# Counting VectorE's semaphore steps over a whole lap, and waiting for loads by a register, in a streaming mean-subtraction kernel

## The chip, the cores and the metric

One core of a Trainium2 chip. The metric is the device time of one execution in microseconds (us), of the slowest core; here there is one core. Three chips were used; the kernel before took 1285.1 to 1285.3 us (medians) on each.

## The reference

```python
B, S, D = 8, 4096, 2112          # x: float32, 276.8 MB
x_r = x.reshape(B, S // 4, 4, D)
pooled = x_r.mean(axis=2)
return (x - np.repeat(pooled, 4, axis=1)).astype(np.float32)
```

From every group of four rows its mean row is subtracted. All of x is read once and as many bytes are written.

## The kernel before

A tile is 128 groups, one per partition, 4 x 2112 = 8448 fp32 columns, 4.325 MB. There are 64 tiles and six SBUF slots. SyncE issues the loads; VectorE adds the four rows in three steps into a sum tile (in SBUF and PSUM by turns), then one wide instruction computes rows - sum/4 in place; ScalarE issues the stores. A load for a slot waits for the slot's store of the lap before.

```python
def reduce_tile(b, parity):
    rows = slots[b].rearrange("p (f d) -> p f d", f=STRIDE)
    s = s_ps if parity else s_sb
    add = nc.vector.tensor_add(out=s[:], in0=rows[:, 0, :], in1=rows[:, 1, :])   # L60
    add._wait_ge(load_sems[b], 16)
    add.then_inc(load_sems[b], -16)          # taken back
    add = nc.vector.tensor_add(out=s[:], in0=s[:], in1=rows[:, 2, :])            # L63
    add.wait_op(load_sems[b], 0, "sem-eq")
    add.then_inc(step_sem)
    add = nc.vector.tensor_add(out=s[:], in0=s[:], in1=rows[:, 3, :])            # L66
    add._wait_ge(step_sem, 1)
    add.then_inc(step_sem, -1)               # taken back
    sub = nc.vector.scalar_tensor_tensor(out=rows, ...)                          # L69
    sub.wait_op(step_sem, 0, "sem-eq")
    sub.then_inc(done_sem)
# ... cut: loads as k = 0..63 on SyncE ...
with nc.vector.Fori(0, laps):                # 10 laps of 6 tiles, then 4 tiles
    for b in range(SLOTS):
        reduce_tile(b, b % 2)
# ... cut: stores on ScalarE, store k waits for done_sem >= k + 1 ...
```

## Time and profile before

| | before |
|---|---|
| time, median of the first 3 runs | 1285.18 us (1285.16 to 1285.22) |
| span of the profiled run | 1283.3 us |
| VectorE busy | 1026.5 us, 80% |
| loads and stores, time of their packets as a share of 16 DMA engines | 50.1% + 50.0% |
| period of a tile in the steady state | 19.97 us |
| VectorE's chain for one tile, from landing to the end of the wide instruction | 16.3 us |

### The profile page before, as it was taken

The numbers are of one execution on the slowest core, as the hardware profiler recorded it, in microseconds if no ns is written. First come the engines' busy times: TensorE is split into PE (matmuls) and PEld (weight loads), VectorE is DVE, ScalarE is ACT, GpSimd is POOL, SyncE is SP. The second block draws the span as 40 slices with busy tenths as digits, with TensorE's granted clock in tenths as the row PEclk, the third lists the DMA queues.
The fourth block names the chain that finished last, engine by engine and source line by source line (L and its number), as shares of the span: only waits on it lengthen the run. The fifth ranks groups of instructions, "written<-read, shape, count | busy, mean of one in ns | idle before, by whom it ended". The sixth has DMA issues, their size and how long they took to land.

```text
span 1283.3 us, 591 instructions
## 1 busy us (share of the span) xinstructions
DVE 1026.5 (80%) x256; POOL 0.2 (0%) x4
## 2 busy tenths in 40 slices
DVE  5998788787787877878778787787887878878775
POOL 0000000000000000000000000000000000000000
DMA  9999999999999999999999999999999999999999
GB/s 404 421 437 433 428 438 432 428 438 437 431 430 438 432 428 438 437 429 432 438 432 428 438 436 429 433 438 432 428 438 435 429 434 438 432 428 438 434 427 404
DMA packets 18433, 553.66 MB, mean 431 GB/s; under 512 B 2048, under 2 KB 2048, under 8 KB 2048
## 3 DMA queue, kind: packets, MB, share of 16 engines
q1 hardware_dynamic: 9216, 276.83, 50.1%
q10 hardware_dynamic: 9216, 276.83, 50.0%
q14 instruction: 1, 0.01, 0.0%
HBM read 276.82 MB, written 276.82 MB: 431 GB/s over the span
## 4 chain that ended last, share of the span: by engine, by line
DVE 71%; another core or an unknown queue 23%; issue 3%; DMA 1%; DVEq 0%; SPq 0%
DVE slot L69 36%; DVE s_ps L66 6%; DVE s_ps L60 6%; DVE s_ps L63 6%; DVE s_sb L66 6%; DVE s_sb L63 6%; DVE s_sb L60 6%; DMA slot<-in_x_dram 1%; DVEq L66 0%; DVEq L60 0%; DVEq L90 0%; SPq L131 0%; SPq L82 0%
## 5 line engine op out<-in xcount | busy, mean ns | idle before, releaser
L69 DVE SCALAR_TENSOR_TENSOR slot<-s_sb,slot 128x8448 f32<-128x8448 f32 x32 | 286.6, 8957 | 1.1
L69 DVE SCALAR_TENSOR_TENSOR slot<-s_ps,slot 128x8448 f32<-128x8448 f32 x32 | 286.6, 8957 | 1.1
L60 DVE TENSOR_TENSOR s_sb<-slot 128x2112 f32<-128x2112 f32 x32 | 75.4, 2357 | 121.7 <-DMA slot<-in_x_dram 121.7
L60 DVE TENSOR_TENSOR s_ps<-slot 128x2112 f32<-128x2112 f32 x32 | 75.7, 2366 | 109.2 <-DMA slot<-in_x_dram 109.2
L66 DVE TENSOR_TENSOR s_ps<-s_ps,slot 128x2112 f32<-128x2112 f32 x32 | 75.7, 2367 | 3.3
L66 DVE TENSOR_TENSOR s_sb<-s_sb,slot 128x2112 f32<-128x2112 f32 x32 | 75.5, 2358 | 3.3
L63 DVE TENSOR_TENSOR s_ps<-s_ps,slot 128x2112 f32<-128x2112 f32 x32 | 75.7, 2366 | 1.1
L63 DVE TENSOR_TENSOR s_sb<-s_sb,slot 128x2112 f32<-128x2112 f32 x32 | 75.4, 2358 | 1.1
L120 POOL MEMSET const-bfloat16-1.0<- 128x1 bf16 x1 | 0.1, 102 | 0.0
L120 POOL MEMSET const-uint8-127<- 128x1 uint8 x1 | 0.1, 101 | 0.0
L120 POOL MEMSET const-float32-0.0<- 128x1 f32 x1 | 0.1, 99 | 0.2 <-issue 0.2
L120 POOL MEMSET const-float32-1.0<- 128x1 f32 x1 | 0.1, 98 | 0.0
## 6 DMA issues: line engine op xcount, KB each, us to landing
slot<-in_x_dram SPq DMA_DIRECT2D x64, 4224.0 KB, 59.7
out_dram<-slot ACTq DMA_DIRECT2D x64, 4224.0 KB, 43.7
```

The lines of the kernel that those rows point to most:

```text
L60: add = nc.vector.tensor_add(out=s[:], in0=rows[:, 0, :], in1=rows[:, 1, :])
L63: add = nc.vector.tensor_add(out=s[:], in0=s[:], in1=rows[:, 2, :])
L66: add = nc.vector.tensor_add(out=s[:], in0=s[:], in1=rows[:, 3, :])
L69: sub = nc.vector.scalar_tensor_tensor(out=rows, in0=s[:, None, :].to_broadcast([P, STRIDE, D]), scalar=-1.0 / STRIDE, in1=rows, op0=mybir ...
L120: nc = _bacc.Bacc("TRN2", target_bir_lowering=False, num_devices=1)
```

## The change

The intent is to have nothing to take back in a tile. The step counter only rises during a lap (18 adds) and is reduced once at its end; the load semaphores only rise, and the first add waits for a value that a register holds for the lap. The core of the diff:

```diff
-    def reduce_tile(b, parity):
+    def reduce_tile(b, landed):
...
-        add._wait_ge(load_sems[b], 16)
-        add.then_inc(load_sems[b], -16)
-        ... three adds written out, the third with then_inc(step_sem, -1)
+        done = b * adds                      # adds = 3
+        for f in range(1, STRIDE):
+            first = rows[:, 0, :] if f == 1 else s[:]
+            add = nc.vector.tensor_add(out=s[:], in0=first, in1=rows[:, f, :])
+            if f == 1:
+                add._wait_ge(load_sems[b], landed)
+            else:
+                add._wait_ge(step_sem, done + f - 1)
+            add.then_inc(step_sem)
-        sub.wait_op(step_sem, 0, "sem-eq")
+        sub._wait_ge(step_sem, done + adds)
...
-        with nc.vector.Fori(0, laps):
+        with nc.vector.Fori(0, laps) as lap:
+            landed = nc.vector.to_reg(16 * lap + 16)
             for b in range(SLOTS):
-                reduce_tile(b, b % 2)
+                reduce_tile(b, landed)
+            nc.vector.wait_ge(step_sem, SLOTS * adds).then_inc(step_sem, -SLOTS * adds)
```

More of the change, by code (lines that the diff above doesn't have):

```diff
@@ L31 @@
     G = (B * S) // STRIDE
-    assert STRIDE == 4 and S % STRIDE == 0 and G % P == 0
+    assert S % STRIDE == 0 and G % P == 0
     n = G // P
@@ L53 @@
     done_sem = tc.alloc_semaphore("done")
-    def reduce_tile(b, parity):
+    adds = STRIDE - 1
+    def reduce_tile(b, landed):
         rows = slots[b].rearrange("p (f d) -> p f d", f=STRIDE)
-        s = s_ps if parity else s_sb
-        add = nc.vector.tensor_add(out=s[:], in0=rows[:, 0, :], in1=rows[:, 1, :])
-        add._wait_ge(load_sems[b], 16)
-        add.then_inc(load_sems[b], -16)
-        add = nc.vector.tensor_add(out=s[:], in0=s[:], in1=rows[:, 2, :])
-        add.wait_op(load_sems[b], 0, "sem-eq")
-        add.then_inc(step_sem)
-        add = nc.vector.tensor_add(out=s[:], in0=s[:], in1=rows[:, 3, :])
-        add._wait_ge(step_sem, 1)
-        add.then_inc(step_sem, -1)
+        s = s_ps if b % 2 else s_sb
+        done = b * adds
[7 more added lines that the diff above has]
+            add.then_inc(step_sem)
         sub = nc.vector.scalar_tensor_tensor(
@@ L88 @@
             load.then_inc(load_sems[b], 16)
-        with nc.vector.Fori(0, laps):
+        with nc.vector.Fori(0, laps) as lap:
+            landed = nc.vector.to_reg(16 * lap + 16)
             for b in range(SLOTS):
-                reduce_tile(b, b % 2)
+                reduce_tile(b, landed)
+            nc.vector.wait_ge(step_sem, SLOTS * adds).then_inc(step_sem, -SLOTS * adds)
         for b in range(rest):
-            reduce_tile(b, b % 2)
+            reduce_tile(b, 16 * (laps + 1))
         for k in range(n):
```

## The prediction

> **What bounds the kernel now.** I read the page from the top: busy shares, slices, DMA queues. 64 tiles of 128 x 8448 fp32 pass through six slots; SyncE issues loads, VectorE (DVE) does three adds and one wide multiply-add, ScalarE issues stores.
>
> ```profile
> span 1283.3 us, 591 instructions
> ## 1 busy us (share of the span) xinstructions
> DVE 1026.5 (80%) x256; POOL 0.2 (0%) x4
> ...
> DMA  9999999999999999999999999999999999999999
> ...
> q1 hardware_dynamic: 9216, 276.83, 50.1%
> q10 hardware_dynamic: 9216, 276.83, 50.0%
> ```
>
> VectorE is busy 80% of the span. The DMA row is 9 in all 40 slices, and the two rings (q1 loads, q10 stores) together take 100.1% of the time of 16 DMA engines. That is the first sign that transfers are the bound. Occupancy of 16 engines can mislead, so I check the rate. The starts of the first add in two steady tiles 32 apart (613.31 and 1252.19 us on the timeline) give a period of 638.88 / 32 = 19.965 us. In it one tile of 4.325 MB is loaded and one is stored: 8.651 MB / 19.965 us = 433 GB/s.
>
> Next, the groups of instructions: what VectorE waits for.
>
> ```profile
> L60 DVE TENSOR_TENSOR s_sb<-slot 128x2112 f32<-128x2112 f32 x32 | 75.4, 2357 | 121.7 <-DMA slot<-in_x_dram 121.7
> L60 DVE TENSOR_TENSOR s_ps<-slot 128x2112 f32<-128x2112 f32 x32 | 75.7, 2366 | 109.2 <-DMA slot<-in_x_dram 109.2
> L66 DVE TENSOR_TENSOR s_ps<-s_ps,slot 128x2112 f32<-128x2112 f32 x32 | 75.7, 2367 | 3.3
> ```
>
> Ahead of each tile's first add (L60) VectorE stands idle for the load, 121.7 + 109.2 = 230.9 us in all; the other three instructions of a tile wait for next to nothing. One steady tile in the chain of waits:
>
> ```profile
> 609.53 3.68 another core or an unknown queue
> 613.21 0.03 issue
> 613.24 0.02 DVEq L60
> 613.26 0.04 issue
> 613.31 2.38 DVE s_ps L60
> 615.68 0.02 issue
> 615.71 2.38 DVE s_ps L63
> 618.08 0.03 issue
> 618.11 0.02 DVEq L66
> 618.13 0.04 issue
> 618.18 2.38 DVE s_ps L66
> 620.55 0.02 issue
> 620.58 8.96 DVE slot L69
> ```
>
> The page's chain puts 71% on VectorE, which invites the wrong conclusion. The chain alternates: 16.3 us of VectorE, then 3.68 us with no name. The group lines name it: the load. So VectorE has about 3.7 us of slack in every 19.97 us. Its work sits in the chain because a tile does pass through it, but the pace is set by the transfers. A closed loop of six slots could also be limited by latency, not by rate: with nothing queued a tile would need about 12.4 us of load (the fastest landing), 16.3 us of VectorE and 13.9 us of store (the fastest landing), 42.6 us in all, or 7.1 us per tile over six slots. The period is 19.97 us, so the slots are not short; the medians of 59.7 us (load) and 43.7 us (store) from issue to landing are mostly queueing. Both rings always hold work.
>
> **The two ends** must be looked at apart, for there a later VectorE could show. At the head six loads are queued at once, about 60 us of transfer, and the first store is issued at 29.7 us: the engines never run dry. At the tail the windows of 2 us show:
>
> ```profile
> 1266.00:1268.00 2.00, 2.00 (x1) 0.00 (x0) 1.00 1.21 524
> 1268.00:1270.00 2.00, 0.42 (x1) 0.00 (x0) 1.00 0.86 372
> 1270.00:1272.00 2.00, 0.00 (x0) 0.00 (x0) 1.00 1.06 456
> ```
>
> The last two columns are the DMA share and GB/s. The last store is issued at 1268.4 us, when VectorE ends, and lands 13.9 us later. Alone at 433 GB/s it would need 4.325 MB / 433 = 10.0 us, so about 3.9 us of other stores (and completion) still stand ahead of it. The rate does not dip before it joins. A last store issued a little earlier only queues.
>
> [...]
>
> **The change part by part.** *Removed*: two take-backs per tile (load semaphore by 16, step semaphore by 1) and the equality waits for them. The trace has a separate 21 ns semaphore instruction ahead of L60 and of L66, x64 each. The gap before L66 is 0.03 + 0.02 + 0.04, about 0.10 us by start times (618.18 - 618.08); that before L63 or L69, without one, is 0.02 to 0.03. One is worth about 0.07 us, two 0.15 us a tile, 64 tiles 9.6 us of VectorE time. *Added*: in each of ten laps a register value, a wait for 18 adds and a subtraction of 18. The instruction order shows one more instruction at the lap's start and a wait merged into the loop's register step. Register steps of the loop take 40 ns and its branch 56 ns now; three or four such are some 0.2 us a lap, 2 us in all. They can run beside the lap's last wide instruction (8.96 us), because the last add is done before that starts. Each first add now compares against a register[...]. *Unchanged*: the four VectorE instructions, all 128 DMAs, slots, store waits, 553.66 MB.
>
> VectorE's sum: -9.6 + (0 to 2)[...] = -9.6 to -1.2 us of time not counted as busy. The tile goes from 16.28 to about 16.15 us. All of this is inside 3.7 us of slack, so the wait for the load grows by as much: 230.9 us becomes 232 to 241 us. On the path that sets the end: 0. At the head stores are issued 0.1 to 0.7 us earlier and meet a busy queue: 0.
>
> **The rivals.** (1) *VectorE's time is on the path*, as the 71% suggests: then 9.6 us come off, 1275.6 us, 0.7% and still within 2%. Against it: idle for the load ahead of 59 of 64 first adds, full DMA in all slices. (2) *The new wait replaces the old ones and costs more*: a register wait, or a lap's end that drains VectorE. It would have to exceed 3.7 us per tile, or build up beyond the slack and the queue, to show; even 1 us fully exposed in each of ten laps makes 1295 us, under 1%. Nothing in the trace takes that long on the sequencer: 21 to 56 ns apiece. (3) *Shifted stores change how loads and stores mix*, hence the DMA rate. The slices scatter between 428 and 438 GB/s by turns, averaging 433; an overall shift of 0.1% (1.3 us) is thinkable either way, with nothing in favour of a direction.
>
> **Range and chances.** The transfers set the time, so I take 1285.1 us. Three runs lie within 0.06 us, so the range comes from rival 3 and a small share of rival 1: 1284.2 to 1286.0 us. For 2% the time must move 25.7 us, over twice what the whole saving could give and far more than the lap's work could cost. Chances: faster 0.005, within 2% 0.985, slower 0.01.
>
> **What would show it.** Right: DMA share still 9 everywhere, 433 GB/s steady, period 19.97 us; no semaphore instruction ahead of the first and third add; the gap before the third add down from 0.10 to about 0.03 us; VectorE still 1026.5 us busy; its load waits up by 1 to 10 us; span 1283 us. Wrong: a period that moves with VectorE's chain (rival 1), a sequencer gap of microseconds at each lap's first add (rival 2), or the same bytes at another rate (rival 3).

Cut from the prediction is what no trace or run showed: the term for a first add that compares against a register. VectorE's sum came to -9.6 to -1.2 us with that term; the terms left, -9.6 and 0 to 2, come to -9.6 to -7.6 us. The lower ends of "232 to 241 us" and "up by 1 to 10 us" hold the cut term too: without it the wait for loads would become 238.5 to 240.5 us, 7.6 to 9.6 us more. The 1285.1 us does not rest on it, for the prediction counts all of VectorE's time as slack. That the adds keep their length is shown by the pages: the groups' means are 2357 to 2367 ns before and 2358 to 2367 ns after.

## The result, and the profile after

The changed kernel took 1284.87 us (median of 6 runs, 1284.78 to 1285.14), the kernel before 1285.20 us in 6 runs. The ratio is 0.9998, 95% interval 0.9985 to 1.0011: the same. (Ratios here are the mean time of one kernel's fast runs over that of the other's fast runs of the same rounds, so not quite the ratio of the medians quoted.)

The page of the changed kernel:

```profile
span 1283.3 us, 483 instructions
## 1 busy us (share of the span) xinstructions
DVE 1026.5 (80%) x256; POOL 0.2 (0%) x4
...
DMA  9999999999999999999999999999999999999999
...
q1 hardware_dynamic: 9216, 276.83, 50.1%
q10 hardware_dynamic: 9216, 276.83, 50.0%
```

108 instructions fewer than before (591), the same busy time, the same span, the same two DMA queues (called rings below: q1 carries the loads, q10 the stores) at 100% of the engines.

The groups, with the last two fields being busy us with mean ns, and idle us ahead with what ended it:

```profile
L63 DVE TENSOR_TENSOR s_sb<-slot 128x2112 f32<-128x2112 f32 x32 | 75.5, 2358 | 123.7 <-DMA slot<-in_x_dram 123.7
L63 DVE TENSOR_TENSOR s_ps<-slot 128x2112 f32<-128x2112 f32 x32 | 75.7, 2367 | 112.1 <-DMA slot<-in_x_dram 112.1
L63 DVE TENSOR_TENSOR s_ps<-s_ps,slot 128x2112 f32<-128x2112 f32 x64 | 151.4, 2366 | 2.2
```

The wait for the load is 123.7 + 112.1 = 235.8 us, 4.9 us more than before.

One steady tile of the changed kernel in the chain of waits (start, us, what), the same tile as the prediction shows of before:

```profile
609.98 3.81 another core or an unknown queue
613.79 0.02 issue
613.81 2.38 DVE s_ps L63
616.19 0.02 issue
616.21 2.38 DVE s_ps L63
618.59 0.02 issue
618.61 2.38 DVE s_ps L63
620.99 0.02 issue
621.01 8.96 DVE slot L69
```

The two DVEq pieces of 0.02 us, the separate semaphore instructions, are gone. From the end of the wait to the end of the wide instruction the tile takes 629.97 - 613.79 = 16.18 us, against 629.54 - 613.21 = 16.33 us: 0.15 us saved. The wait in front of it grew from 3.68 to 3.81 us. The saving is real and the load takes it back in the same tile.

The absolute times hold something more. This first add starts at 613.81 us, *later* than 613.31 us before, although VectorE became faster. The start of the run shows where that sets in. Before:

```profile
29.60 2.36 DVE L60 TENSOR_TENSOR s_ps<-slot 128x2112 f32<-128x2112 f32 x1
...
85.23 8.96 DVE L69 SCALAR_TENSOR_TENSOR slot<-s_sb,slot 128x8448 f32<-128x8448 f32 x1
94.22 2.37 DVE L60 TENSOR_TENSOR s_ps<-slot 128x2112 f32<-128x2112 f32 x1
```

After:

```profile
29.38 2.36 DVE L63 TENSOR_TENSOR s_ps<-slot 128x2112 f32<-128x2112 f32 x1
...
84.73 8.96 DVE L69 SCALAR_TENSOR_TENSOR slot<-s_sb,slot 128x8448 f32<-128x8448 f32 x1
94.73 2.37 DVE L63 TENSOR_TENSOR s_ps<-slot 128x2112 f32<-128x2112 f32 x1 [1.04 <-DMA slot<-in_x_dram]
```

In the first five tiles VectorE does not wait for loads, and its gain adds up: the fifth wide instruction begins 0.50 us earlier (84.73 against 85.23), so stores start earlier. Yet the sixth tile's first add, which hardly waited before, now waits 1.04 us and begins 0.51 us later (94.73 against 94.22), and from there every load is complete 0.6 us later.

It is tempting to say that the earlier stores pushed the loads back, but the trace does not bear that out. Averaged over the time from 300 to 1200 us, the bytes moved so far are the same in both kernels: 168.26 MB of loads against 168.30 before, 155.05 MB of stores in each. The trace records 16 completions for every transfer (2048 for 128 transfers). Midway, the first of a load's 16 comes at 632.71 us against 632.68 before; the last comes 1.04 us after it instead of 0.49, with the other fifteen within 0.53. So one completion of the 16 comes half a microsecond behind the others (633.75 us, the one ahead of it 633.24), and VectorE waits for the last: its first add starts at 633.77 us. Whether the change causes this is not shown: there is one profile of each kernel, and two variants of the changed kernel in experiment 4 (1.8 us after the wide instruction, 0.5 us in the chain) have no such straggler.

The last store is issued at 1268.9 instead of 1268.4 us and lands 13.5 instead of 13.9 us later. The end stays.

### The profile page after: what moved, and what is told of

Read it like the earlier page. It is cut to its first block, busy times and chain, and to the rows that moved or that the text cites. A ratio compares the mean times of both kernels' runs of the same rounds, so it can differ in the third digit from the quotient of the medians.

```text
span 1283.3 us, 483 instructions
## 1 busy us (share of the span) xinstructions
DVE 1026.5 (80%) x256; POOL 0.2 (0%) x4
## 2 busy tenths in 40 slices
DMA packets 18432, 553.66 MB, mean 431 GB/s; under 512 B 2048, under 2 KB 2048, under 8 KB 2048
## 3 DMA queue, kind: packets, MB, share of 16 engines
q1 hardware_dynamic: 9216, 276.83, 50.1%
## 4 chain that ended last, share of the span: by engine, by line
DVE 73%; another core or an unknown queue 24%; DMA 1%; issue 1%; DVEq 0%; SPq 0%
DVE slot L69 38%; DVE s_ps L63 18%; DVE s_sb L63 18%; DMA slot<-in_x_dram 1%; DVEq L90 0%; SPq L133 0%; SPq L82 0%
## 5 line engine op out<-in xcount | busy, mean ns | idle before, releaser
L63 DVE TENSOR_TENSOR s_sb<-slot 128x2112 f32<-128x2112 f32 x32 | 75.5, 2358 | 123.7 <-DMA slot<-in_x_dram 123.7
L63 DVE TENSOR_TENSOR s_ps<-slot 128x2112 f32<-128x2112 f32 x32 | 75.7, 2367 | 112.1 <-DMA slot<-in_x_dram 112.1
L63 DVE TENSOR_TENSOR s_sb<-s_sb,slot 128x2112 f32<-128x2112 f32 x64 | 150.9, 2358 | 2.2
```

What stands on the lines that cost most here:

```text
L63: add = nc.vector.tensor_add(out=s[:], in0=first, in1=rows[:, f, :])
```

## The experiments

Twelve kernels were run. The theory: the transfers set the time, and VectorE's gain disappears in its wait for loads. Rival 1: VectorE's chain is on the path, as the chain view's 73% of the changed kernel suggests. (Rival 2 of the prediction, a costly register wait, is tested in experiment 3; rival 3, another DMA rate, comes up in experiment 4.) Diffs are shortened. "Wrong result" below means a kernel that was meant to compute something else.

### 1. VectorE's work taken away (wrong result)

```diff
-  tensor_add(out=s[:], in0=first, in1=rows[:, f, :])      # and the wide instruction over 8448 columns
+  tensor_add(out=s[:, :8], in0=..., in1=rows[:, f, :8])   # and the wide instruction over 4 x 8
```

> The changed kernel with all four VectorE instructions cut to 8 columns (wrong result on purpose): same loads, stores, waits and order, but VectorE's chain per tile falls from 16.2 us to about 1 us. Theory (the transfers set the time): the time stays at 1284 to 1286 us; the first store starts near 15 us instead of 29.5 us, the loads then share the engines from earlier on, so the last load lands 10 to 20 us later than 1252.6 us, and the end does not move. Rival 1 (VectorE's chain is on the path, as its 73% share of the chain suggests): about 15 us per tile come off, or at least 15 us at the two ends: 1270 us or far less.

Measured: 1285.49 us (median of 4, 1285.01 to 1285.92), ratio 1.0001. VectorE was busy 45.0 us instead of 1026.5 us, and the time did not move. The timeline of this kernel, first and last tile:

```profile
14.15 77.37 ACTq L100 DMA_DIRECT2D out_dram<-slot  x5
...
1269.40 0.18 DVE L63 TENSOR_TENSOR s_ps<-slot 128x8 f32<-128x8 f32 x1 [19.19 <-DMA slot<-in_x_dram]
```

The first store is issued at 14.15 us, 15.4 us earlier than in the changed kernel (29.50 us); the last first add begins at 1269.40 us, 16.7 us later than there (1252.69 us). What stores gain, loads lose: averaged from 300 to 1200 us, the stores have moved 3.50 MB more than in the changed kernel and the loads 3.55 MB less, and the end stays. Rival 1 falls.

### 2. Fewer bytes, the same VectorE work (wrong result)

```diff
-  store = nc.scalar.dma_start(out=og[k * P:(k + 1) * P], in_=slots[b][:])
+  store = nc.scalar.dma_start(out=og[k * P:(k + 1) * P, :3 * D], in_=slots[b][:, :3 * D])
```

> The changed kernel with each store cut to three of the four rows of a group (wrong result on purpose): VectorE does the same work, the bytes fall by one eighth, 69.2 MB. Theory: the time falls by 69.2 MB / 433 GB/s = 160 us, to about 1125 us (1115 to 1140), a period of 17.5 us, with VectorE's tile of 16.16 us still inside it. Rival 1: the time does not move by more than a few us.

Measured: 1128.18 us, ratio 0.878. An eighth of the bytes less, 12.2% of the time less. The stores' ring fell to 42.8% of 1126.3 us = 482 us of all engines, three quarters of the 642 us (50.0% of 1283.3) that it had. Time goes with bytes.

### 3. VectorE made the bound, and the two parts of the change one by one (wrong results)

In these four, loads after the first lap and all stores move two of the four rows, about 10 us per tile. The first is the kernel before, the second the changed kernel; the third and fourth carry one part of the change each:

```diff
# all four
-  load = nc.sync.dma_start(out=slots[b][:], in_=xg[k * P:(k + 1) * P])
+  wide = 2 * D if lap else W
+  load = nc.sync.dma_start(out=slots[b][:, :wide], in_=xg[k * P:(k + 1) * P, :wide])   # store: :2 * D
# third: steps counted over the lap (two per tile), load semaphores still taken back
-  add._wait_ge(step_sem, 1);  add.then_inc(step_sem, -1)
+  add._wait_ge(step_sem, done + 1);  add.then_inc(step_sem)
# fourth: load wait by register, the steps still taken back in every tile
-  add._wait_ge(load_sems[b], 16);  add.then_inc(load_sems[b], -16)
+  add._wait_ge(load_sems[b], landed);  add.then_inc(step_sem)
-  add._wait_ge(step_sem, 1);  add.then_inc(step_sem, -1)      # third add
+  add._wait_ge(step_sem, 2);  add.then_inc(step_sem, -2)
```

> The kernel before with loads (after the first lap) and stores cut to two of four rows (wrong result on purpose): transfers of about 10 us per tile, so VectorE is the bound. At the head of the unchanged kernel, where VectorE is not waiting either, a tile takes 16.13 us (13.47 to 29.60 us). Expected: 13.5 + 64 x 16.13 + about 9 = 1055 us (1045 to 1065). It is the yardstick for the next three.

> The changed kernel with the same cut, VectorE-bound. Theory: where no load is awaited, the take-back ahead of the first add runs beside the wide instruction of the tile before and was already free; only the one ahead of the third add was exposed. A tile takes 16.06 us (13.32 to 29.38 us at the head), so 64 x 0.07 = 4.5 us less than the first of these four, a ratio of 0.9957; about 1050 us. Rival A: both take-backs count, 64 x 0.15 = 9.6 us, ratio 0.991. Rival B: the lap's close and the register wait cost what is saved: ratio 1.000.

> Only the step counter is counted over the lap; the load semaphores are taken back as before; VectorE-bound by the same cut. Theory: this part has the whole saving, 4.5 us less than the first of these four (ratio 0.9957), and equals the second within 0.5 us. Rival A: half of 9.6 us, 4.8 us less, with the other half in the fourth kernel.

> Only the load wait goes by register; the step counter is taken back in every tile as before; VectorE-bound by the same cut. Theory: nothing, within 0.5 us of the first of these four, since the take-back ahead of the first add lay beside the wide instruction. Rival A: 4.8 us less. Rival B: a register wait that costs 0.1 us would show as 6 us more.

| VectorE-bound kernel | median us (5 runs) | against the first |
|---|---|---|
| before | 1055.07 | |
| changed | 1050.32 | -4.75 |
| only the step counter over the lap | 1050.43 | -4.64 |
| only the load wait by register | 1054.76 | -0.31 |

The spread within a row is at most 0.43 us. The theory's four numbers hold: where VectorE is the bound, the change is worth 4.75 us, 0.45%, and the step counter has nearly all of it. The take-back of the load semaphore cost nothing there, since it ran beside the wide instruction of the tile before. (At the head of the kernel before, where VectorE does not wait either, the semaphore instruction ran at 23.34 us, inside the wide instruction of 20.72 to 29.68 us.) The tiles themselves show it. VectorE-bound kernel before:

```profile
515.62 2.38 DVE s_ps L63
518.00 0.03 issue
518.02 0.02 DVEq L66
518.04 0.04 issue
518.09 2.38 DVE s_ps L66
```

VectorE-bound changed kernel:

```profile
513.62 2.38 DVE s_ps L63
515.99 0.02 issue
516.02 2.38 DVE s_ps L63
```

From the end of the second add to the start of the third: 0.09 us against 0.03 us by these pieces, 104 against 34 ns on average of the 64 tiles. The difference, 0.07 us, by 64 tiles is 4.5 us.

### 4. How much slack is there really?

The trace shows 3.8 us of idle VectorE per tile. Two runs fill it with extra adds in the chain (1.77 us each by their pages), one within it and one beyond:

```diff
+  # after the first add, EXTRA times, each a step of the chain (about 1.79 us)
+  more = nc.vector.tensor_add(out=extra[:], in0=rows[:, 0, :1536], in1=rows[:, 1, :1536])
+  more._wait_ge(step_sem, at);  more.then_inc(step_sem)
```

> The changed kernel with one more add of 1536 columns per tile on VectorE, in the chain between the first and second add, about 1.79 us, so that a tile takes about 17.9 us: inside the 3.8 us of slack. Theory: 1284.8 to 1285.6 us, the wait for loads shrinks by about 1.8 us per tile. Rival 1: 64 x 1.79 = 114 us more, 1400 us.

> The same with three extra adds per tile, about 5.37 us, a tile of 21.4 us on VectorE: more than the 19.97 us of its transfers. Theory: VectorE becomes the bound and the time is 13.3 + 64 x 21.43 + about 14 = 1399 us (1385 to 1410), and the DMA share falls below 9 tenths. If there were more slack than the 3.8 us that the trace shows, it would be less than that. Rival 1: 64 x 5.37 = 344 us more, 1629 us.

Three extra adds: 1400.80 us, as the theory has it (1399): VectorE is the bound, busy 97%. But the expected fall of the DMA share below 9 tenths did not come: the DMA row is 9 in 37 of 40 slices, and from 480 to 960 us the engines are 97% busy at 403 GB/s. The 1284 us that the packets of the changed kernel take would alone be 92% of 1399, and here they take longer. So a full DMA row alone does not show that transfers set the pace; the rate of 433 GB/s and experiments 1 and 2 do.

One extra add: **1321.83 us** (1318.79 to 1324.26), ratio 1.0277. Neither the theory (1285) nor rival 1 (1400). The expectation failed. The page of that run:

```profile
span 1322.3 us, 547 instructions
...
q1 hardware_dynamic: 9216, 276.83, 50.7%
q10 hardware_dynamic: 9216, 276.83, 48.6%
...
L66 DVE TENSOR_TENSOR s_sb<-slot 128x2112 f32<-128x2112 f32 x32 | 75.4, 2357 | 88.0 <-DMA slot<-in_x_dram 88.0
L66 DVE TENSOR_TENSOR s_ps<-slot 128x2112 f32<-128x2112 f32 x32 | 75.7, 2366 | 72.3 <-DMA slot<-in_x_dram 72.3
```

VectorE still waits 160 us for loads, so it is not the bound. The same bytes took longer: the load ring's packets 50.7% of 1322.3 us = 670 us, against 50.1% of 1283.3 = 643 us; the store ring's did not (643 and 642 us). The rest, 0.7% of the span, is engines that stood empty. So a theory was needed for how VectorE, inside its slack, slows the transfers. Three were put against each other: the extra add issues the *stores later*; its SBUF reads get in the way of the load packets (M); or the longer backlog at the head upsets the transfers for good (H). A copy within PSUM, of the same length, tells them apart: in the same place (no SBUF access), or after the wide instruction (no later store, the backlog at the head remains).

```diff
+  more = nc.vector.tensor_copy(out=extra[:], in_=extra[:])    # PSUM to PSUM, 1.76 us
```

> The one extra add inside the slack cost 37 us against expectation; its trace shows load packets that took longer, though the DMA share stayed near 100%. Here the changed kernel gets an extra copy of 1536 columns from PSUM to PSUM (about 1.8 us) after the wide instruction of each tile, so that in the steady state it runs while VectorE waits for a load and no store is issued later. New theory (it is the later issue of the stores that upsets the transfers): 1284 to 1287 us. Rival H (the backlog at the head, where VectorE is late in this run too, upsets them for good): about 1320 us. Rival M (SBUF reads of the extra add slow the load packets): 1285 us, as this copy reads no SBUF.

> The same PSUM copy, but in the chain between the first and second add, where the extra add stood: stores are issued about 1.8 us later, without any SBUF access added. New theory (later stores): 1310 to 1330 us, as with the extra add. Rival M (SBUF reads): 1284 to 1286 us.

After the wide instruction: 1284.89 us, ratio 0.9997. In the chain: 1322.76 us, ratio 1.0294. M and H fall: what matters is that the chain ahead of the store is delayed, and the later store is the likeliest reason. That is not shown alone, for the copy in the chain also moves the last two adds and the wide instruction, with their SBUF accesses, against the transfers; no run delayed only the store's issue on ScalarE. VectorE was busy 88% of the span in the first of the two and 86% in the second: its load is not what matters.

Two smaller delays were to show the shape:

> The extra add in the chain again, but of 330 columns, about 0.5 us. If the loss grows in proportion to the delay: 37 x 0.5 / 1.79 = 10 us, 1295 us. If there is a threshold above it (the kernel before, 0.15 us later than the changed one, shows no loss): 1284 to 1286 us.

> The PSUM copy in the chain between the first and second add, cut to 810 columns, about 1.0 us: stores issued about 1.0 us later, between the 0.5 us that left three of four runs at 1285 us and the 1.8 us that cost 37 us. If there is an abrupt edge, the runs lie either at 1285 to 1288 us or at 1310 us and more, or in both groups; if the loss grows evenly from 0.5 us on, about 1300 us. If the whole of the 3.8 us were usable slack, as the prediction took it, 1285 us.

The add of 330 columns, 0.51 us: 1284.97, 1287.86, 1285.09 and 1284.73 us, so no loss but in one run. The copy of 810 columns, 1.01 us: **1393.64 us** (median of 6, 1390.89 to 1401.42), ratio 1.0853. The number falls under one of the three expectations (an abrupt edge, with runs at 1310 us and more), but none had that a smaller delay costs three times as much as the larger one. Its page:

```profile
span 1391.6 us, 548 instructions
...
q10 hardware_dynamic: 9216, 276.83, 49.8%
q1 hardware_dynamic: 9216, 276.83, 46.8%
```

Here the store ring's packets take 693 us (49.8% of 1391.6), 51 us more than in the changed kernel, the load ring's 651 us, and 3.4% of the span the engines are empty.

What such runs have in common can be counted in the trace. A transfer's 128 large packets (33,792 bytes, one partition of a tile) at 1251 ns each are 160 us of packet time, and the last store of the kernel before lands 13.9 us after its issue: over 11 at a time, so one transfer is spread over most of the 16 engines. For each transfer 16 completions are recorded. From the first to the last of the 16, midway through the run:

| kernel | time us | spread of a load's 16 completions |
|---|---|---|
| before | 1285 | 0.5 us |
| changed | 1285 | 1.0 us |
| no VectorE work | 1285 | 1.7 us |
| 1.8 us after the wide instruction | 1285 | 0.6 us |
| 0.5 us in the chain | 1285 | 0.5 us |
| 1.8 us in the chain (add) | 1322 | 11.6 us |
| 1.8 us in the chain (PSUM copy) | 1323 | 8.9 us |
| 1.0 us in the chain | 1394 | 47.8 us |

In the runs at 1285 us the completions stay together (0.5 to 1.7 us), and after the head all but a few of the large packets take those 1251 ns (from 120 us on, all but 42 of 14,880 in the kernel before and all of 14,882 in the changed one). In the slow ones the completions drift apart from the first tiles on and do not come together again while loads run. They do so in two ways. With 1.8 us all 16 spread out, and the spread grows through the run from about 0.5 to 20 us. With 1.0 us thirteen completions of a load midway lie within 0.6 us of each other, and three come 45 to 48 us later. In these runs 12 to 19% of the packets of one ring take over 5% longer (the load ring in the 1.8 us runs, the store ring in the 1.0 us run). Longer packets alone are no mark of it: with three extra adds, 8% of the load ring's and 6% of the store ring's do too, at spreads of 0.2 to 5.3 us. Nor is little slack: in experiment 2 VectorE waited only 1.3 us per tile, and the spread was 0.4 us. VectorE and the next load wait for the last of the 16: in the changed kernel the first add starts 0.02 us after a load's last completion (633.75 to 633.77 us), and the next load is issued 0.02 us after a store's (613.58 to 613.59 us). In the slow runs engines are empty for 0.7 to 3.4% of the span; that these are the ones whose part of a transfer is done early is an estimate and was not counted. That the completions drift apart in the runs with 1.0 or 1.8 us in the chain (8.9 to 47.8 us), and not with 1.8 us behind it (0.6 us), is shown. *Why* a given delay does this, why 1.0 us does it more than 1.8 us, and why some packets then take longer, stays open. The runs of 0.5 and 1.0 us were also on different chips and with different extra instructions, so they mark no exact edge; the 1.8 us case was seen on two chips.

No version here beats both kernels: experiment 1 shows that even without VectorE's work the time is 1285 us, and every byte moved is needed. Other ways of moving the same bytes were not tried.

## Why the prediction was right

**The bound**: right. The prediction took the time from the transfers, 1285.1 us in a range of 1284.2 to 1286.0; measured 1284.87. Experiments 1 and 2 confirm the reason: the time stays without VectorE's work and follows the bytes.

**The saving per tile**: 0.15 us predicted, 0.15 us measured (16.33 to 16.18 us). (The prediction's own "16.28 to about 16.15" takes off only 0.13; a slip.) The gap ahead of the third add fell from 0.10 to 0.03 us as said. **The register wait**: landing to first add is 0.02 us (613.79 to 613.81), and the part alone was worth -0.31 us in 64 tiles. **The lap's close**: in the changed chain its pieces last from 101.97 to 102.39 us, beside a wide instruction that began at 101.93 and runs 8.96 us: hidden, as said. From the close of the first lap:

```profile
102.04 0.05 DVEq L90
102.09 0.03 issue
102.12 0.06 DVEq L90
102.19 0.14 issue
102.33 0.06 DVEq L90
```

**The wait for loads**: 232 to 241 us predicted, 235.8 measured; the terms left after the cut would have said 238.5 to 240.5. And the sum has another make-up than the prediction's. Before, the 230.9 us held the load semaphore's take-back, for that stood between the landing and the first add; its 0.08 us per tile only changed its name to waiting. What moved over from elsewhere is the gap ahead of L66, 6.6 us before, and 2.2 us now as one of the groups of adds (4.4 us less), and VectorE ends 0.4 us later, because its loads are complete later: 4.4 + 0.4 = 4.8 of the 4.9 us.

**The head**: "stores are issued 0.1 to 0.7 us earlier and meet a busy queue: 0" held: the first store is issued 0.21 us earlier, and the end stays. That loads are complete half a microsecond later, for one of 16 completions, it did not see. **Rival 3**, another rate by another mix, did not come from this change (the slices lie between 426 and 437 GB/s, the ends apart, against 427 to 438 before), but the experiments show that the same bytes can move at another rate (419 and 398 GB/s on average, against 431) and that this is far larger than the 0.1% given to it: 37 us for 1.8 us more ahead of the stores, 108 us for 1.0 us. That the mix of loads and stores is the cause is not shown.

**One statement fails** beyond this change: that a new cost "would have to exceed 3.7 us per tile" to show. The idle time ahead of the first add is not free for any use. The right part of it is that work *not* ahead of a store cost nothing here (1.76 us after the wide instruction, 1284.89 us). That the prediction held fits with the change moving stores earlier, for experiment 1 moved them much earlier (the first by 15.4 us) without harm (1285.49 us). It gave no such reason: its chance of 0.01 for slower rested on slack that a change in the other direction would not have had. On this point it was right by luck.

The 0.33 us between the medians (0.03%) lies inside the interval of the ratio and is not explained.

## What to carry to other kernels

Here, where the DMA rings filled the whole span at 433 GB/s, a saving on a compute engine only lengthened its wait (230.9 to 235.8 us); read such a saving's worth from a run in which that engine is the bound (here 4.75 us, from one of the two parts). A busy engine's share of the chain view does not show that it sets the pace: VectorE had 73% here, and the time stayed at 1285 us when its work was cut from 1026.5 to 45.0 us. Idle time in this pipeline was not all slack: 1.0 us of extra work ahead of each store cost 108 us, while 1.76 us behind the work that releases the store cost nothing, so put extra work there and measure it. The share of time that DMA engines are busy stayed near full while their rate fell (97% at 403 GB/s with three extra adds), so look at the rate too.
